# A 7-stage transformer block pair on one core: one phase order for all Winograd quads, a raised estimate of accumulating DMAs, splits three units ahead, squares summed on VectorE, gate tiles in the other row

## The chip, the core and the metric

The kernel runs on one core of a Trainium2 chip. Its engines each work through a queue of their own in order: TensorE (PE; PEld is its weight load), VectorE (DVE), ScalarE (ACT), GpSimd (POOL) and SyncE (SP), which only issues transfers. They are coupled by semaphores. The metric is the device time of one execution in microseconds; lower is better. All weights stay in HBM and are streamed through on-chip memory once.

## The reference

All arithmetic is fp32, for a sequence of 512 tokens with 1024 channels. Two blocks run one after the other. Cut to its main lines:

```python
h = x + concat(gla(n), mla(n)) @ w_out             # n = rms_norm(x); stage mix
h = h + square(relu(rms_norm(h) @ w_mlp_up)) @ w_mlp_down      # mlp: 1024 -> 4096 -> 1024
h = h + (p @ w_ple_proj) * sigmoid(rms_norm(h) @ w_ple_gate + b)   # ple
x = h
x = x + pool_mixer(rmsnorm(x))                     # pool: trailing means
x = x + conv_ffn(rmsnorm(x), ...[0])               # ffn0: 1024 -> 2816 -> 1024
x = x + chunk_attention(rmsnorm(x))                # att
x = x + conv_ffn(rmsnorm(x), ...[1])               # ffn1

def conv_ffn(h):
    a = h @ w_gate
    a = causal_depthwise_conv3(a) + conv_b
    return (silu(a) * (h @ w_val)) @ w_out
```

The change is in the three stages mlp, ffn0 and ffn1.

## The kernel before

`x` is kept transposed as 8 tiles of 128 channels by 512 tokens. A stage's norm doesn't scale its input: the products run on `x` times the gain, and each product is multiplied by the row `R` (one over the root mean square of each token) when it leaves PSUM. `square` sums the squares of the 8 tiles (`sq`), `stats` turns the sum into `ms` (a matmul `pst`, then VectorE), `r` (POOL's power), `dg` (ACT), `psr` (a matmul) and `R` (ACT).

**Weights.** They come in units of 128x1024 fp32 (512 KB). SP loads a unit into one of 7 slots `ws`. `split_unit` makes two float32r tiles of it: ACT copies two halves of 128x512 to `wh`, VectorE takes `wl` = `ws` - `wh`. There are 4 such pairs, so the split of unit n needs the pair of unit n-4, which TensorE must have finished. Each product is three matmuls (`mm3`): high by high, low by high, high by low. `splitter` runs at most `lazy` units ahead of TensorE's current one.

**Quads.** The up products of mlp, ffn0 and ffn1 take four feature tiles at a time (a Quad) by a Winograd scheme with seven products instead of eight. They are named in PHASES by position: 0 b11, 1 b21, 2 n3, 3 n2, 4 n1, 5 b22, 6 t4. Each is one unit and 24 matmuls of 128x256 into a PSUM tile `pq0` to `pq4`. n3, n2 and b22 share one `ws` tile ("sum"): SP loads source block 0, a DMA on POOL's queue adds block 2 for n3, and after n3's split another adds block 3 for n2, and after n2's split a third adds block 1 for b22. n1's tile ("low") is a load and one accumulating DMA. On the input side b11 and b22 use the tile's halves `xs`, n3 and n2 use `xc`, t4 uses `xt`. Copies `c1`, `u2`, `u4` by ACT take partial results out of `pq0`, so the next phase that needs `pq0` waits for them.

The order of the phases in a quad was one of three tuples at line 55: FIRST for a stage's first quad, LAST for the last quad of each ffn, MOST for all others (`quads[q].order`, line 1264). The first four feature tiles of a stage are done plainly (`first_tiles`, PSUM tiles `pf`, four units of 24 matmuls 128x512). After each group of quads come its downs: `pdn`, units of 24 matmuls that take the activations `y` (as `yh`, `yl`); `units_quads` places them between phases of the next group's quads, after the positions in the tuple at line 1267.

**ffn rows.** A quad's results make two rows of two tiles: row 0 is complete at the last position, row 1 one position earlier. In `finish` (line 1614) row 0 is the gate (convolution in `fb`, then Silu) and row 1 the value, which is multiplied with it to `y`.

**What sets the order.** The program is written by tasks with priorities (`spawn`, `drive`). `Pace` estimates when each engine and tile is free, `drive` takes the best task that could start by then, and the order so found is fixed in each engine's queue. An instruction that waits holds everything behind it on its engine. `Pace.note` (line 95) has an accumulating DMA's tile ready 4.8 us after its issue. All instructions are recorded through one helper and carry its line, L148, so they are told apart by their tiles.

Of the kernel before, what the change touches and what calls it, by code (L numbers as in the profile page):

```python
# [53 lines left out]

FIRST, MOST, LAST = (0, 1, 2, 3, 6, 4, 5), (2, 0, 1, 3, 6, 4, 5), (2, 0, 1, 3, 5, 4, 6)
# [17 lines left out]
class Pace:  # L73
# [21 lines left out]
    def note(self, engine, op, args, kw):  # L95
# [39 lines left out]
        for x in outs:  # L135
            self.ready[x.tensor.name] = start + cost + (2.0 if engine == "sync" else 4.8 if op == "dma_start" else 0.08)
# [22 lines left out]
class Norm:  # L159


    def __init__(self, gain):
        self.gain, self.xs, self.acc, self.count = gain, [None] * KD, None, 0
        self.ms = self.r = self.R = None
        self.low, self.blocks = [None] * 4, {p[0]: [None] * 4 for p in PHASES}
        self.plain = False
# [11 lines left out]
class Quad:  # L178


    def __init__(self, src):
        self.src, self.tile, self.order = src, {}, MOST


class Block:
# [86 lines left out]
    def plan_loads(self):  # L272

        self.loads, known = [], set()
        for n, u in enumerate(self.units):
            if not isinstance(u[0], str):
                self.loads.append((n, n, u[0], u[1], None, ()))
            elif u[1] not in known:
                known.add(u[1])
                for name, block, at, more in LOADS:  # L280
                    at = -5 if u[1].order == FIRST and name == "sum" else at
                    self.loads.append((n + at, u[1], u[1].src[block], 1024, name, more))
        self.loads.sort(key=lambda e: e[0])
# [203 lines left out]
    def square(self, norm, x, row=True, late=True):  # L487
        nc = self.nc
        sq = self.slot("sq")
        nc.scalar.activation(sq, x, AF.Square)  # L490
        if norm.acc is None:
            norm.acc = sq
        else:
            (nc.vector if late and norm.count > 5 else nc.gpsimd).tensor_add(norm.acc, norm.acc, sq)
        norm.count += 1
        if norm.count == KD:
            self.spawn(self.stats(norm, row), -4)
# [754 lines left out]
    def units_quads(plain, src, downs, sizes):  # L1252
# [3 lines left out]
        for g, n in enumerate(sizes):  # L1256
            for i in range(n):
                left -= 1
                if q < 0:
                    order.append((q, 0))  # L1260
                    units += plain
                else:
                    most = 0 if q == 0 else -(-len(wait) // (n - i)) if left else len(wait) - 2
                    quads[q].order = FIRST if q == 0 else MOST if left or most > 0 else LAST
                    for at, ph in enumerate(quads[q].order):
                        order.append((q, ph))
                        units.append(("quad", quads[q], ph))
                        for _ in range(((5, 2, 6, 3) if i else (5, 6, 4, 3))[:min(most, len(wait))].count(at)):
                            order.append(wait[0][:2])
                            units.append(wait.pop(0)[2])  # L1270
                q += 1
# [36 lines left out]
    def quads(self, norm, order, quads, sizes, last, after, take, finish, late=None):  # L1308
# [8 lines left out]
        for what, i in order:  # L1317
# [8 lines left out]
            own = quads[what].order != MOST  # L1326
# [26 lines left out]
            if i == quads[what].order[-1]:  # L1353
# [255 lines left out]
    def ffn(self, L, norm, after):  # L1609
# [4 lines left out]
        def finish(acts, rows, r, i):  # L1614
            f = 2 * count[r]
            count[r] += 1
            if r == 0:
                yield rows[0]
                made = []
                for w in range(2):  # L1620
                    a, b = rows[0][w], self.slot("fb")
# [10 lines left out]
            for w, b in enumerate(gates.pop((i, id(acts)))):  # L1632
                y = rows[1][w]
# [159 lines left out]
    def main(self, stages):  # L1793
# [13 lines left out]
        for i, st in enumerate(stages):  # L1807
# [11 lines left out]
            self.help = self.HELP[st in self.QUADS]  # L1819
            yield from run[st](norm, after)  # L1820
            self.lazy, self.most = self.LAZY[1], self.NL
# [88 lines left out]
def lay_out(x, p, positions, attn_norm, w_in, gla_gate_w2, gla_gate_b, gla_out_norm, mla_q_norm, mla_w_uq, mla_kv_norm,  # L1910
# [30 lines left out]
    for L in range(2):  # L1941
        both = np.stack([w.reshape(DM, -1, 2, P) for w in (ffn_w_gate_2[L], ffn_w_val_2[L])], 2)
# [45 lines left out]
```

## Time and profile before

| | us |
|---|---|
| median of 3 runs (lowest, highest) | 1703.4 (1700.95, 1705.31) |
| the profiled execution | 1700.45 |
| its span | 1698.7 |
| PE busy | 1638.1 (96%) |
| VectorE busy | 1260.0 (74%) |
| ACT busy | 887.4 (52%) |
| POOL busy | 280.1 (16%) |
| mean granted clock of TensorE | 0.983 of full speed |

In the timeline each row is: start in us, length in us, engine, line, operation, output <- input with size, count, and in brackets the idle time ahead of it and whose result ended it. A row with xN stands for N instructions, its length is from the first to the last.

### The profile page before, as it was taken

Reading aid. Unit: us, or ns where it says so; the run is one execution under the profiler, and the core shown is the slowest. Engines: PE = TensorE matmul, PEld = TensorE weight load, DVE = VectorE, ACT = ScalarE, POOL = GpSimd, SP = SyncE. Lnnn points to the kernel's source line nnn. Section 1 sums busy time; section 2 is a strip of 40 time slices with the busy share of each in tenths; the row PEclk is TensorE's granted clock in tenths of the full one; section 3 lists DMA queues with packets and bytes.
Section 4 is the critical chain, followed back from the end, with each engine's and each line's share of the span. In section 5 each row is a group of like instructions: output and inputs, shape, how many; then the busy total and the mean of one; then the engine's idle time right before and its main releaser. Section 6 shows DMA issues by size and latency. Waiting matters only on the chain. (4 is left out here: it accounts for less than half of the span.)

```text
span 1698.7 us, 27854 instructions
## 1 busy us (share of the span) xinstructions
PE 1638.1 (96%) x10676; PEld 1467.1 (86%) x10676; DVE 1260.0 (74%) x2435; ACT 887.4 (52%) x1730; POOL 280.1 (16%) x310
## 2 busy tenths in 40 slices
PE   9999999999999999979999998999999989999998
PEld 7878778899999888869999997998988779999987
DVE  7976868766666667878787767576668788787766
ACT  6745456544444465654454534476666554455532
POOL 3432302100000022211011100321322211111100
PEclk9999999999999999979999998999999989999999
DMA  7101223556666333366777753322231467777741
GB/s 275 50 26 38 98 77 100 158 160 164 165 164 174 134 99 116 82 155 174 186 187 183 180 156 107 120 83 68 76 100 63 112 164 184 176 201 180 184 128 50
DMA packets 66391, 224.87 MB, mean 132 GB/s; under 512 B 7617, under 2 KB 9554, under 8 KB 66258
## 3 DMA queue, kind: packets, MB, share of 16 engines
q1 hardware_dynamic: 50706, 166.46, 28.0%
q0 software_dynamic: 15552, 56.63, 19.3%
q8 instruction: 84, 1.38, 0.3%
q14 instruction: 49, 0.40, 0.1%
HBM read 220.96 MB, written 2.10 MB: 131 GB/s over the span
## 5 line engine op out<-in xcount | busy, mean ns | idle before, releaser
L148 ACT ACTIVATE wh<-ws 128x512 fp32r<-128x512 f32 x690 | 392.1, 621 | 258.2 <-PE pdn L148 125.7
L148 DVE TENSOR_TENSOR wl<-ws,wh 128x512 fp32r<-128x512 f32 x667 | 437.4, 698 | 110.9 <-ACT wh L148 110.8
L148 PE MATMUL pq<-xsl,wh 128*128 128x256 f32 x864 | 244.5, 283 | 0.0
L148 PE MATMUL pq<-xsh,wl 128*128 128x256 f32 x864 | 244.5, 283 | 0.0
L148 PE MATMUL pq<-xsh,wh 128*128 128x256 f32 x864 | 244.4, 283 | 0.0
L148 DVE TENSOR_TENSOR x<-x,pdn 128x512 f32<-128x512 f32 x177 | 119.8, 680 | 78.3 <-PE pdn L148 77.9
L148 POOL DMA_DIRECT2D ws<-in_w_f x80 | 70.6, 937 | 611.7 <-DVE wl L148 279.2
L148 PEld LDWEIGHTS pq<-xsh,wh 128*128 128x128 f32 x864 | 165.7, 192 | 1.3
L148 PEld LDWEIGHTS pq<-xsl,wh 128*128 128x128 f32 x864 | 165.6, 192 | 1.2
L148 PEld LDWEIGHTS pq<-xsh,wl 128*128 128x128 f32 x864 | 165.6, 192 | 0.0
L148 PE MATMUL pdn<-yh,wh 128*128 128x512 f32 x352 | 142.9, 406 | 14.8 <-ACT yh L148 14.7
L148 PE MATMUL pdn<-yl,wh 128*128 128x512 f32 x352 | 142.8, 406 | 5.7 <-DVE yl L148 5.6
L148 PE MATMUL pq<-xch,wh 128*128 128x256 f32 x432 | 126.5, 293 | 15.2 <-ACT wh L148 9.6
L148 PE MATMUL pdn<-yh,wl 128*128 128x512 f32 x352 | 140.8, 400 | 0.0
L148 PE MATMUL pq<-xch,wl 128*128 128x256 f32 x432 | 125.4, 290 | 0.4 <-DVE wl L148 0.4
L148 PE MATMUL pq<-xcl,wh 128*128 128x256 f32 x432 | 125.0, 289 | 0.0
L148 PE MATMUL paq<-wh,xsh 128*128 128x256 f32 x384 | 111.3, 290 | 1.9 <-DVE akk L148 1.2
L148 PE MATMUL paq<-wl,xsh 128*128 128x256 f32 x384 | 108.6, 283 | 0.0
L148 PE MATMUL paq<-wh,xsl 128*128 128x256 f32 x384 | 108.5, 283 | 0.0
L148 PEld LDWEIGHTS pq<-xch,wh 128*128 128x128 f32 x432 | 85.8, 199 | 18.1 <-ACT wh L148 10.8
L148 PE MATMUL pdn<-hh,wh 128*128 128x512 f32 x256 | 99.9, 390 | 0.0
L148 PE MATMUL pdn<-hl,wh 128*128 128x512 f32 x256 | 99.9, 390 | 0.0
(332 smaller groups left out, 3941.3 us busy)
## 6 DMA issues: line engine op xcount, KB each, us to landing
ws<-in_w_f SPq DMA_DIRECT2D x108, 512.0 KB, 3.8
ws<-in_w_f POOLq DMA_DIRECT2D x80, 512.0 KB, 5.5
ws<-in_w_fo SPq DMA_DIRECT2D x44, 512.0 KB, 4.8
ws<-in_w_up SPq DMA_DIRECT2D x39, 512.0 KB, 3.8
ws<-in_w_down SPq DMA_DIRECT2D x32, 512.0 KB, 4.1
ws<-in_w_up POOLq DMA_DIRECT2D x28, 512.0 KB, 5.8
ws<-in_w_out SPq DMA_DIRECT2D x8, 512.0 KB, 3.2
ws<-in_w_gate SPq DMA_DIRECT2D x8, 512.0 KB, 3.2
```

The costliest lines, as they stand in the source:

```text
L148: return call(*args, **kw)
```

## The change

Six edits. One tuple ORDER = (2, 0, 1, 3, 6, 4, 5) takes the place of FIRST, MOST and LAST; what hung on the order (an own PSUM tile for b22 in the first and the last quad, the early load in the first) hangs on two flags. The planner takes 7.0 us instead of 4.8 for an accumulating DMA. In mlp, ffn0 and ffn1 `lazy` is 3 instead of 2. In the norms of these stages VectorE adds all squares; POOL had added the first ones. In the ffns gate and value are packed the other way round, so the gate is row 1. In quad 1 of the ffns (the first quad with downs of the plain tiles) the downs stand after positions 5 and 6 rather than 2 and 5.

```diff
@@ -51,8 +51,7 @@
 PHASES = (("b11", 0, True, "a11"), ("b21", 1, True, "a12"), ("n3", 2, True, "sum"), ("n2", 0, False, "sum"),
           ("n1", 0, False, "low"), ("b22", 0, False, "sum"), ("t4", 3, True, "a22"))
 
-
-FIRST, MOST, LAST = (0, 1, 2, 3, 6, 4, 5), (2, 0, 1, 3, 6, 4, 5), (2, 0, 1, 3, 5, 4, 6)
+ORDER = (2, 0, 1, 3, 6, 4, 5)
 
 LOADS = (("sum", 0, -3, (2,)), ("a11", 0, 1, ()), ("a12", 1, 2, ()), ("low", 2, 2.5, (3,)), ("a22", 3, 4, ()))
 
@@ -133,7 +132,7 @@
                 if x.tensor.name in self.open:
                     self.open[x.tensor.name] = (self.step, start + cost + 0.08)
         for x in outs:
-            self.ready[x.tensor.name] = start + cost + (2.0 if engine == "sync" else 4.8 if op == "dma_start" else 0.08)
+            self.ready[x.tensor.name] = start + cost + (2.0 if engine == "sync" else 7.0 if op == "dma_start" else 0.08)
 
 
 class Engine:
@@ -161,6 +160,7 @@
 
     def __init__(self, gain):
         self.gain, self.xs, self.acc, self.count = gain, [None] * KD, None, 0
+        self.only = gain in ("mlp_norm", "ffn0", "ffn1")
         self.ms = self.r = self.R = None
         self.low, self.blocks = [None] * 4, {p[0]: [None] * 4 for p in PHASES}
         self.plain = False
@@ -179,7 +179,7 @@
 
 
     def __init__(self, src):
-        self.src, self.tile, self.order = src, {}, MOST
+        self.src, self.tile, self.first, self.own = src, {}, False, False
 
 
 class Block:
@@ -278,7 +278,7 @@
             elif u[1] not in known:
                 known.add(u[1])
                 for name, block, at, more in LOADS:
-                    at = -5 if u[1].order == FIRST and name == "sum" else at
+                    at = -5 if u[1].first and name == "sum" else at
                     self.loads.append((n + at, u[1], u[1].src[block], 1024, name, more))
         self.loads.sort(key=lambda e: e[0])
 
@@ -491,7 +491,7 @@
         if norm.acc is None:
             norm.acc = sq
         else:
-            (nc.vector if late and norm.count > 5 else nc.gpsimd).tensor_add(norm.acc, norm.acc, sq)
+            (nc.vector if late and (norm.count > 5 or norm.only) else nc.gpsimd).tensor_add(norm.acc, norm.acc, sq)
         norm.count += 1
         if norm.count == KD:
             self.spawn(self.stats(norm, row), -4)
@@ -1261,11 +1261,12 @@
                     units += plain
                 else:
                     most = 0 if q == 0 else -(-len(wait) // (n - i)) if left else len(wait) - 2
-                    quads[q].order = FIRST if q == 0 else MOST if left or most > 0 else LAST
-                    for at, ph in enumerate(quads[q].order):
+
+                    quads[q].first, quads[q].own = q == 0, q == 0 or left + most == 0
+                    for at, ph in enumerate(ORDER):
                         order.append((q, ph))
                         units.append(("quad", quads[q], ph))
-                        for _ in range(((5, 2, 6, 3) if i else (5, 6, 4, 3))[:min(most, len(wait))].count(at)):
+                        for _ in range(((5, 2, 6, 3) if i and q > 1 else (5, 6, 4, 3))[:min(most, len(wait))].count(at)):
                             order.append(wait[0][:2])
                             units.append(wait.pop(0)[2])
                 q += 1
@@ -1323,7 +1324,7 @@
                 yield from self.first_tiles(norm, take, acts[0])
                 continue
             block, acc, first, _ = PHASES[i]
-            own = quads[what].order != MOST
+            own = quads[what].own
             if i == 5 and own:
                 acc, first = 4, True
             if quad is None:
@@ -1350,7 +1351,7 @@
             self.used(ps[acc])
             if i != 2:
                 self.spawn(self.quad_step(i, ps, quad, own), -3)
-            if i == quads[what].order[-1]:
+            if i == ORDER[-1]:
                 ps = quad = None
 
     def quad_step(self, i, ps, quad, own):
@@ -1614,11 +1615,11 @@
         def finish(acts, rows, r, i):
             f = 2 * count[r]
             count[r] += 1
-            if r == 0:
-                yield rows[0]
+            if r == 1:
+                yield rows[1]
                 made = []
                 for w in range(2):
-                    a, b = rows[0][w], self.slot("fb")
+                    a, b = rows[1][w], self.slot("fb")
                     s.activation(b, a, AF.Identity, scale=cw[2](f + w), bias=self.col(f"cb{L}", f + w))
                     yield [b]
                     v.scalar_tensor_tensor(b[:, 1:], a[:, :T - 1], cw[1](f + w), b[:, 1:], op0=OP.mult, op1=OP.add)
@@ -1630,7 +1631,7 @@
                 return
             yield lambda: (i, id(acts)) in gates
             for w, b in enumerate(gates.pop((i, id(acts)))):
-                y = rows[1][w]
+                y = rows[0][w]
                 yield [b, y]
                 self.mul(y, y, b)
                 yield [y]
@@ -1817,8 +1818,9 @@
                 nxt = None
                 after = self.store
             self.help = self.HELP[st in self.QUADS]
+            self.lazy = self.LAZY[st not in ("mix", *self.QUADS)]
             yield from run[st](norm, after)
-            self.lazy, self.most = self.LAZY[1], self.NL
+            self.most = self.NL
             norm = nxt
 
 
@@ -1939,7 +1941,7 @@
     o["w_proj"] = np.ascontiguousarray(proj.reshape(2, 4, P, 256).transpose(0, 2, 1, 3)).reshape(2, P, 1024)
     o["w_pool"] = np.ascontiguousarray(pool_w_2[0].reshape(2, 2, 2, P, 256).transpose(0, 3, 1, 2, 4)).reshape(2, P, 1024)
     for L in range(2):
-        both = np.stack([w.reshape(DM, -1, 2, P) for w in (ffn_w_gate_2[L], ffn_w_val_2[L])], 2)
+        both = np.stack([w.reshape(DM, -1, 2, P) for w in (ffn_w_val_2[L], ffn_w_gate_2[L])], 2)
         o[f"w_f{L}_0"], o[f"w_f{L}"] = pack_first(both[:, 0]), pack_quads(both[:, 1:])
         o[f"w_fo{L}"] = pack_downs(ffn_w_out_2[L], 2, QG2)
     q, k, v = np.split(attn_wqkv_2[0], 3, axis=1)
```

POOL's queue around the start of ffn0, before: `sq` are sums of squares, `ws_6653` is the "sum" tile of quad 0 (second and third accumulate), `ws_7237` that of quad 1, `ws_7411` its "low", `ws_7644` the "sum" of quad 2.

```order
L148 TENSOR_TENSOR sq_7168<-sq_7168,sq_7207 128x512
L148 DMA ws_7237<-in_w_f0 128x1024
L148 TENSOR_TENSOR sq_7168<-sq_7168,sq_7247 128x512
L148 TENSOR_TENSOR sq_7168<-sq_7168,sq_7264 128x512
L148 TENSOR_TENSOR sq_7168<-sq_7168,sq_7280 128x512
L148 DMA ws_7411<-in_w_f0 128x1024
L148 TENSOR_TENSOR r_7453<-ms_7451,mhalf_72 128x4
L148 DMA ws_6653<-in_w_f0 128x1024 x2
L148 DMA ws_7644<-in_w_f0 128x1024
L148 DMA ws_7237<-in_w_f0 128x1024 x2
```

The same place of POOL's queue after: `ws_6653` is again quad 0's "sum", `ws_7236` quad 1's, `ws_7421` its "low", `ws_7647` quad 2's "sum".

```order
L147 TENSOR_TENSOR xn_7187<-xn_7187 128x256
L147 TENSOR_TENSOR xn_7211<-xn_7211 128x256
L147 DMA ws_7236<-in_w_f0 128x1024
L147 DMA ws_6653<-in_w_f0 128x1024
L147 DMA ws_7421<-in_w_f0 128x1024
L147 TENSOR_TENSOR r_7471<-ms_7469,mhalf_72 128x4
L147 DMA ws_6653<-in_w_f0 128x1024
L147 DMA ws_7647<-in_w_f0 128x1024
L147 DMA ws_7236<-in_w_f0 128x1024 x2
```

The second accumulate of quad 0's "sum" (for n2) moved ahead of `r`; the second of quad 1's still stands behind the first of quad 2's.

ACT's queue at the same place, before: `wh_7469` is the split of n3, `wh_7567` of n2, `wh_7638` of b22; `R` is the norm's row.

```order
L148 ACTIVATE wh_7469<-ws_6653 128x512 x2
L148 ACTIVATE xsh_7164<-xn_7170 128x256
L148 ACTIVATE xsh_7180<-xn_7187 128x256
L148 ACTIVATE xsh_7203<-xn_7211 128x256
L148 ACTIVATE xsh_7243<-xn_7251 128x256
L148 ACTIVATE dg_7506<-ident_65,r_7453 128x128 x4
L148 ACTIVATE c1_7514<-pq0_7465 128x512
L148 ACTIVATE R_7559<-psr_7557 128x512
L148 ACTIVATE wh_7567<-ws_6653 128x512 x2
L148 ACTIVATE wh_7574<-ws_7053 128x512 x2
L148 ACTIVATE wh_7582<-ws_6976 128x512 x2
L148 ACTIVATE u2_7626<-pq0_7465 128x512
```

And after: `wh_7473` is the split of n2 (n3's, `wh_7312`, stands further ahead), `wh_7513` of t4, `wh_7556` of n1, `wh_7641` of b22, `wh_7650` of the next quad's n3.

```order
L147 ACTIVATE wh_7473<-ws_6653 128x512 x2
L147 ACTIVATE xsh_7164<-xn_7170 128x256
L147 ACTIVATE xsh_7180<-xn_7187 128x256
L147 ACTIVATE xsh_7203<-xn_7211 128x256
L147 ACTIVATE xsh_7247<-xn_7255 128x256
L147 ACTIVATE wh_7513<-ws_7053 128x512 x2
L147 ACTIVATE dg_7542<-ident_65,r_7471 128x128 x4
L147 ACTIVATE c1_7554<-pq0_7512 128x512
L147 ACTIVATE wh_7556<-ws_6976 128x512 x2
L147 ACTIVATE R_7603<-psr_7601 128x512
L147 ACTIVATE u2_7626<-pq0_7512 128x512
L147 ACTIVATE wh_7641<-ws_6653 128x512 x2
```

The splits of n2, t4 and n1 moved ahead of `R`.

PE's queue in quad 1 of ffn0, before, at the end of b21 (`pq1`):

```order
L148 MATMUL pq1_7812<-xsl_7326,wh_7733 128x256
L148 MATMUL pq1_7812<-xsh_7325,wl_7734 128x256
L148 MATMUL pdn_7839<-yh_7867,wh_7774 128x512
L148 MATMUL pdn_7839<-yl_7868,wh_7774 128x512
L148 MATMUL pdn_7839<-yh_7867,wl_7775 128x512
```

The same place after; `wh_7841` is n2's.

```order
L147 MATMUL pq1_7804<-xsl_7345,wh_7709 128x256
L147 MATMUL pq1_7804<-xsh_7344,wl_7710 128x256
L147 MATMUL pq0_7773<-xch_7377,wh_7841 128x256
L147 MATMUL pq0_7773<-xcl_7378,wh_7841 128x256
L147 MATMUL pq0_7773<-xch_7377,wl_7842 128x256
```

The first down moved from ahead of n2 to behind n1. Around ffn0's first quad PE's order by units was `pf`, `pst`, `pf`, b11, b21, n3 (18 matmuls), `psr`, n3, n2, t4, n1, b22 and is `pf`, `pst`, n3, b11, b21, n2 (15), `psr`, n2, t4, n1, b22; in ffn1 `psr` now stands in t4, after 12.

ACT's queue in the last quad of ffn1, before: `wh_17880` is the split of n2, `wh_17917` of b22.

```order
L148 ACTIVATE wh_17880<-ws_17426 128x512 x2
L148 ACTIVATE yh_17890<-qr_17668 128x512
L148 ACTIVATE wh_17917<-ws_17426 128x512 x2
L148 ACTIVATE c1_17926<-pq0_17879 128x512
L148 ACTIVATE yh_17928<-qr_17669 128x512
```

And after: `wh_17862` is n2's, `wh_17899` t4's, `wh_17932` n1's, `wh_17963` b22's.

```order
L147 ACTIVATE wh_17862<-ws_17407 128x512 x2
L147 ACTIVATE yh_17882<-qr_17578 128x512
L147 ACTIVATE wh_17899<-ws_17636 128x512 x2
L147 ACTIVATE c1_17930<-pq0_17895 128x512
L147 ACTIVATE wh_17932<-ws_17599 128x512 x2
L147 ACTIVATE wh_17963<-ws_17407 128x512 x2
```

The copy `c1` moved ahead of b22's split.

## Rows read from the trace of the kernel before

**Rows 1.** The page: busy time by engine, and the granted clock in 40 slices.

```profile
PE 1638.1 (96%) x10676; PEld 1467.1 (86%) x10676; DVE 1260.0 (74%) x2435; ACT 887.4 (52%) x1730; POOL 280.1 (16%) x310
...
PEclk9999999999999999979999998999999989999999
```

**Rows 2.** Waits of PE: us in total, times, longest.

```profile
PE pdn L148 <- ACT yh L148: 14.7, 5, 7.2
```

**Rows 3.** Timeline of PE, the matmuls that end its idle stretches.

```profile
298.59 0.39 PE L148 MATMUL pq<-xch,wh 128*128 128x256 f32 x1 [1.82 <-ACT wh L148]
...
719.08 1.12 PE L148 MATMUL psr<-dg,ones 128*128 128x512 f32 x2 [1.46 <-ACT dg L148]
...
724.50 0.39 PE L148 MATMUL pq<-xch,wh 128*128 128x256 f32 x1 [3.58 <-ACT wh L148]
...
753.98 0.79 PE L148 MATMUL pdn<-yh,wh 128*128 128x512 f32 x1 [7.25 <-ACT yh L148]
...
1022.08 0.58 PE L148 MATMUL pq<-xch,wh 128*128 128x256 f32 x1 [2.74 <-ACT c L148]
...
1358.26 0.58 PE L148 MATMUL pq<-xch,wh 128*128 128x256 f32 x1 [4.18 <-ACT wh L148]
...
1385.67 0.80 PE L148 MATMUL pdn<-yh,wh 128*128 128x512 f32 x1 [4.71 <-ACT yh L148]
```

**Rows 4.** Windows of PE alone: length, busy (matmuls), granted clock, DMA share, GB/s.

```profile
724.45:728.60 4.15, 3.89 (x19) 0.59 0.21 25
1022.00:1026.50 4.50, 4.42 (x25) 0.64 0.57 179
1358.20:1363.60 5.40, 5.34 (x25) 0.54 0.39 61
...
753.90:765.20 11.30, 9.32 (x24) 0.62 0.58 128
...
1385.60:1396.55 10.95, 9.42 (x24) 0.62 0.69 145
```

**Rows 5.** The chain that ended last, in ffn1: start, us, what.

```profile
1351.15 6.40 DMA ws<-in_w_f
1359.83 5.71 DMA ws<-in_w_f
...
1367.60 3.24 DMA ws<-in_w_f
1371.94 10.25 DMA ws<-in_w_f
...
1396.60 8.63 PE pq L148 x72
1405.23 5.47 PE pdn L148 x24
```

**Rows 6.** Timeline of ACT in ffn0's quad 1 and ffn1's last quad.

```profile
748.91 2.19 ACT L148 ACTIVATE wh<-ws 128x512 fp32r<-128x512 f32 x4 [4.42 <-DMA ws<-in_w_f]
...
1651.84 1.15 ACT L148 ACTIVATE wh<-ws 128x512 fp32r<-128x512 f32 x2 [6.29 <-DMA ws<-in_w_f]
1652.89 0.58 ACT L148 ACTIVATE c<-pq 128x512 f32<-128x512 f32 x1
```

**Rows 7.** POOL's issues of accumulating DMAs: timelines, and the page's landing times.

```profile
737.97 1.75 POOL L148 DMA_DIRECT2D ws<-in_w_f  x2 [11.03 <-DVE u L148]
...
ws<-in_w_f POOLq DMA_DIRECT2D x80, 512.0 KB, 5.5
```

**Rows 8.** Timelines of VectorE and POOL ahead of ffn0, where squares are added.

```profile
695.27 2.29 DVE L148 SCALAR_TENSOR_TENSOR xc<-xn 128x256 f32<-128x256 f32 x1
...
701.02 0.68 DVE L148 TENSOR_TENSOR sq<-sq 128x512 f32<-128x512 f32 x1
701.63 0.41 DVE L148 SCALAR_TENSOR_TENSOR xc<-xn 128x256 f32<-128x256 f32 x1
...
695.67 4.48 POOL L148 TENSOR_TENSOR sq<-sq 128x512 f32<-128x512 f32 x3
```

## The prediction

> **What bounds the kernel now.** I read the page's busy shares and slices first: TensorE is busy for 96% of the span, and its granted clock dips in only a few slices [rows 1]. So there are two ways to gain: stop an idle stretch of TensorE, or stop the half-speed stretch that follows one. The profiled execution took 1700.45 us (span 1698.7), the median of the three runs is 1703.4; the sum below stands against 1700.45, and since the median is 2.95 above it, I treat a shift of 3 us as uncertain either way. About 0.3%, 5 us, is what a measurement can tell from no change.
>
> The list of TensorE's waits has the downs that wait for ACT's `yh` at its head, 14.7 us in five places [rows 2]. The timeline of TensorE shows where [rows 3]: not in the steady quads, but at the edges of the three quad stages. At 298.59 (mlp's first quad), 724.50 (ffn0's) and 1358.26 (ffn1's) phase n2 starts 1.82, 3.58 and 4.18 us late for its split. At 719.08 `psr` waits 1.46. At 753.98 and 1385.67 the first down of the ffns waits 7.25 and 4.71. At 1022.08 the last quad's n2 waits 2.74 for the copy `c1`, and the last quad of ffn1 does the same.
>
> After each wait the clock falls. The windows over the units behind the waits have a granted clock of 0.54 to 0.64 [rows 4], where the long steady stretches of the chain have 72 matmuls 128x256 in 8.63 us, 0.12 each, and a down's 24 in 5.47 [rows 5]; the level in the slow part is 1.2 GHz instead of 2.4. So ffn0's n2 took 3.89 for 19 matmuls instead of 2.28 (+1.6), ffn1's 5.34 for 25 instead of 3.0 (+2.3), the last quad's 4.42 for 25 (+1.4). The two downs' windows are 11.30 and 10.95 long instead of 5.47: 5.8 and 5.5 more, clock and small gaps inside together.
>
> **The change part by part: what it removes.**
> (a) One order for all quads. n2 needs the tile of n3 after a further accumulating DMA, and that starts only when n3 has been split. With n3 directly ahead of n2 there is no room for it: ffn1's chain shows that DMA from 1351.15 for 6.40 us, n2 right behind it [rows 5]. n3 now stands two phases earlier, and its split three units ahead, so POOL issues n2's DMA ahead of `r` (the order shows it). Two more phases, 5.8 us, plus the issue ahead of `r` exceed every one of the three waits. Gone: 1.8 (mlp), 3.6+1.6 (ffn0), 4.2+2.3 (ffn1).
> (b) `psr` moves from 18 matmuls into the third quad unit to 15 into the fourth; `pf`'s last six matmuls move ahead of it. Net distance behind `pst`: 72+15 against 6 wide ones and 66, so 10.4 us instead of about 9.3; its wait of 1.46 goes for the most part: 1.5. In ffn1 it moves on into t4, where nothing waited before.
> (c) First down of the ffns. ACT sat for 4.42 us in front of a split that waited for an accumulating DMA, at 748.91 [rows 6], and the `yh` that the down needs stood behind it. Now the down comes after n1' instead of ahead of n2', three phases (8.6 us) later; the gate's rows are complete one phase earlier, so its chain over ACT and VectorE runs earlier too. 7.25+5.8 and 4.71+5.5 go: 13.1+10.2 = 23.3.
> (d) Last quads of the ffns: ACT's `c1` copy stood behind a split that had waited 6.29 for its third accumulate, at 1651.84, and was issued at 1652.89 [rows 6]; in the new order the copy is ahead of it and t4 and n1 lie between n2 and b22. 2.74+1.4, twice: 8.2.
> Sum removed: 1.8+5.2+6.5+1.5+23.3+8.2 = 46.5.
>
> **What it adds.**
> (e) A new wait in quad 1 of each ffn. With the down gone from between b21' and n2', TensorE arrives at n2' at once. The order shows n2's second DMA behind the sum DMA of quad 2 in POOL's queue, as before, and that one needs a slot which b22's split of quad 0 frees, then a load (3.24 us at 1367.60), then POOL [rows 5]. Behind the waiting split on ACT are the splits of t4', n1' and the first down, then `yh`; behind POOL's waiting issue stands n2's. In before the pair was issued at 737.97 in ffn0 and n2's part had landed when the split at 748.91 began, 10.9 us on; in ffn1 it took 10.25 [rows 5 to 7].
> Price for ffn1: TensorE stood free at 1385.67−4.71 = 1380.96; with 6.5 taken out above it arrives at 1374.4. The DMA landed at 1371.94+10.25 = 1382.2, with 1.3 for the split 1383.5. If nothing in that chain moved, the gap is 9.1. If it moved by the whole link that n2's DMA was in (1359.83−1351.15 = 8.7), the gap is 0.4. The order puts b22's split behind `R`, six scalings and one subtraction on VectorE, and `R` comes later than before, so half of the link: about 5. For ffn0 the same chain gains the larger wait and I take 4. Then the clock: as behind 1358.26, 2.3 each. Added: 4+5+4.6 = 13.6; bounds 1 to 23.
> (f) Fifteen adds of squares move from POOL to VectorE, five per stage: 5 x 0.68 = 3.4 us more per stage, if nothing else changes [rows 8]. Against it: while POOL had its three adds of 4.48 us, an `xc` step of VectorE took 2.29 instead of 0.41, 1.9 more beside three adds [rows 8]. For five adds that is 3.1 back if all do so: bounds 0.3 to 3.4 lost per stage on VectorE. TensorE sees it only through `xc` for n3 (now the first phase) and through `ms`, where (b) leaves about 1 us of margin. I take 0 and keep +10 in all three stages for the range.
> The Trainium skill ("SBUF — State Buffer", Who interferes with whom) says that a VectorE instruction with two SBUF inputs and a GpSimd one that reads SBUF exclude each other; the stretched `xc` row agrees with it; by it (f) would come out even, while the 7 `xn` subtractions that move to POOL would each hold VectorE up once.
> (g) Estimate 7.0 instead of 4.8, and two scalings on ACT instead of VectorE: no instruction is added; they only set the order, which is what (c) and (d) rest on. The accumulating DMAs' median is 5.5 [rows 7], so the planner now puts splits a little late rather than early: cost 0, at most the 1 us that a late split could add in a place where slack is thin. Splits three ahead need a `wh`/`wl` pair that TensorE frees one unit earlier, so ACT waits at most for the unit before: nothing, unless it blocks copies (third rival).
>
> Net: −46.5+13.6 = −32.9; 1700.45−32.9 = 1667.5, so 1667.
>
> **The rivals.**
> First, n2' is hidden: the pair lands 5 us sooner because fewer loads run beside it (a single one takes 5.5 [rows 7], not 10.3). Then nothing is added: 1700.45−46.5 = 1654. For: single landings of 5.5. Against: the two pairs above took twice that.
> The Trainium skill ("DMA: Bandwidth & Descriptors", Anatomy of one DMA — SWDGE (gpsimd) path) gives 2.0 us plus bytes/436e3, an estimate of 3.2 for 512 KB; by that the pair would be in time and this rival would hold. The trace's 5.5 and 10.3 speak against it.
> Second, the first down still waits. Its four `y` come one after another from a chain ACT-VectorE-ACT, and the new wait at n2' also holds the splits ahead of `yh`. If the windows' excess of 5.8 and 5.5 stays although the first wait goes, 11.3 comes back: 1679; with (e) at its upper bounds 1688.
> Third, slower: splits three ahead put ACT, in the 20-odd middle quads too, in front of a split whose DMA hasn't landed, with `c1` or `u2` behind it, as at 1651.84. Each costs 2.74+1.4 = 4.1. Eight such quads eat the gain, ten make it slower by over 5; all 20 give 1667+82 = 1749. Against: the steady quads show no wait now, `c1` moves ahead of those splits where I see it, and the raised estimate makes the planner more careful.
> Fourth, the change doesn't do what it says: the planner's order and the real times differ, the n2 waits only move on to `psr` and t4. Half of 46.5 gone with (e) in full leaves −10: 1690.
>
> **How the numbers follow.** Forecast (1659 to 1675) 0.62; first rival (1650 to 1659) 0.15; second (1675 to 1688) 0.13; fourth (1688 to 1698) 0.05; third 0.05, of which 0.04 is slower by over 5. The range 1652 to 1688 takes the forecast, most of the first and the second, and the bounds of (e) and half of (f). Faster by over 0.3%: 0.94; within: 0.02; slower: 0.04.
>
> **What would show it.** In the changed trace: no wait of n2 in the first quads and no wait of the last quads' n2; the first down starting within 2 us of n1'; a wait of 3 to 6 us at n2' of quad 1 in both ffns with a dip of the clock behind it; VectorE busy by some 5 to 10 us more, POOL by less. The prediction is wrong if middle quads show waits, if `psr` or n3 wait in the ffns for more than 2 us, or if n2' doesn't wait.

## The result, and the profile after

The changed kernel takes 1676.9 us (median of four runs, 1676.23 to 1677.87) against 1702.89 before: a ratio of 0.9847 with a 95% interval of 0.983 to 0.9864, 26 us less. The profiled execution's span is 1675.1 instead of 1698.7. The forecast was 1667.

The page of the changed kernel, first TensorE's and the other engines' busy time, then the granted clock in 40 slices (both answer [rows 1]):

```profile
PE 1633.1 (97%) x10676; PEld 1463.3 (87%) x10676; DVE 1249.1 (75%) x2441; ACT 890.3 (53%) x1732; POOL 265.5 (16%) x302
...
PEclk9999999999999999999999999999999999999999
```

TensorE is busy for 5.0 us less with the same 10676 matmuls, at a mean granted clock of 0.988 instead of 0.983, so this is half-speed time that is gone; the other 18.6 us of the span is idle time that is gone. VectorE, which took over 15 adds, is busy for 10.9 us less; the prediction had expected 5 to 10 more.

TensorE's waits after (us in total, times, longest), for [rows 2]:

```profile
PE pdn L147 <- ACT yh L147: 8.2, 7, 4.0
PE pq L147 <- ACT wh L147: 6.3, 2, 4.2
PE pdn L147 <- DVE yl L147: 4.0, 7, 1.2
...
PE pq L147 <- ACT c L147: 1.0, 2, 0.6
```

Where they are, in the timeline of TensorE (start, length, what, and in brackets the idle time and its releaser), for [rows 3]:

```profile
714.81 0.39 PE L147 MATMUL pq<-xch,wh 128*128 128x256 f32 x1 [0.35 <-ACT c L147]
...
738.11 0.48 PE L147 MATMUL pq<-xch,wh 128*128 128x256 f32 x1 [2.03 <-ACT wh L147]
...
782.94 0.50 PE L147 MATMUL pdn<-yh,wh 128*128 128x512 f32 x1 [0.86 <-ACT yh L147]
784.64 0.50 PE L147 MATMUL pdn<-yl,wh 128*128 128x512 f32 x1 [1.20 <-DVE yl L147]
...
1034.11 0.49 PE L147 MATMUL pdn<-yh,wh 128*128 128x512 f32 x1 [4.03 <-ACT yh L147]
...
1364.58 0.58 PE L147 MATMUL pq<-xch,wh 128*128 128x256 f32 x1 [4.25 <-ACT wh L147]
...
1409.21 0.50 PE L147 MATMUL pdn<-yh,wh 128*128 128x512 f32 x1 [0.86 <-ACT yh L147]
```

All the rows of [rows 3] are gone (a prime, as in n2', marks a phase of quad 1): of the first quads' n2 waits 0.35 is left, in ffn0, `psr` doesn't wait, the first down of quad 1 doesn't wait, nor do the last quads' n2. What is there instead: n2 of quad 1 (738.11 and 1364.58), which was forecast, and something that was not: the first down of quad 2 (782.94 and 1409.21). Each has a stretch of the lower clock behind it. The windows over these units (length, busy with count, granted clock, DMA share, GB/s), first the quad products, then the downs, for [rows 4]:

```profile
738.10:743.00 4.90, 4.86 (x26) 0.65 0.38 52
1364.50:1370.10 5.60, 5.53 (x26) 0.53 0.47 77
```

```profile
780.50:793.30 12.80, 9.57 (x24) 0.73 0.73 164
...
1406.80:1418.70 11.90, 9.51 (x24) 0.71 0.78 173
```

A down of 24 matmuls takes 5.47 undisturbed [rows 5]; here 12.8 and 11.9. So quad 2's first downs cost 7.3 and 6.4 us, together more than the difference between the forecast and the time (9.9).

**Where the down of quad 2 loses it.** ACT's queue in ffn0 (timeline), for [rows 6]:

```profile
760.05 0.82 ACT L147 ACTIVATE fb<-qr,cols 128x512 f32<-128x512 f32 x1 [1.87 <-DVE qr L147]
769.07 1.15 ACT L147 ACTIVATE wh<-ws 128x512 fp32r<-128x512 f32 x2 [8.21 <-DMA ws<-in_w_f]
...
771.17 0.57 ACT L147 ACTIVATE c<-pq 128x512 f32<-128x512 f32 x1
...
772.69 0.62 ACT L147 ACTIVATE fb<-fb 128x512 f32<-128x512 f32 x1
773.21 0.80 ACT L147 ACTIVATE fb<-qr,cols 128x512 f32<-128x512 f32 x1
```

At 760.05 ACT starts quad 1's gate. Its Silu (`fb<-fb`) could follow when VectorE's convolution is done, 766.66 in VectorE's timeline; it runs at 772.69, because ACT stood for 8.21 us in front of quad 2's n2 split. Why that split waits, the chain of the same stretch shows (start, us, what):

```profile
750.51 1.02 DVE wl L147 x2
...
752.43 4.98 DMA ws<-in_w_f
...
757.97 0.54 POOL ws L147
758.51 10.46 DMA ws<-in_w_f
...
769.07 0.09 ACT wh L147
```

POOL's timeline at the same place:

```profile
757.97 1.77 POOL L147 DMA_DIRECT2D ws<-in_w_f  x2 [7.92 <-DVE x L147]
```

VectorE's `wl` frees a slot, SP loads quad 3's "sum" into it (4.98), POOL issues that tile's first accumulate and behind it, in the same moment, n2's for quad 2 (POOL's row has both). The second of the pair has landed 10.46 us later, where the median of all 80 in the ffns is 5.4. POOL's DMA queue (q0) moved 144 packets between 757 and 763.3, none until 764.4 and 144 after that, so the second's transfer began only when the first's was done. So n2's DMA was held twice, by a load that it doesn't need and by a transfer that it doesn't need.

### The profile page after: what moved, and what is told of

Read it like the earlier page. It is cut to its first block, busy times and chain, and to the rows that moved or that the text cites. A ratio compares the mean times of both kernels' runs of the same rounds, so it can differ in the third digit from the quotient of the medians.

```text
span 1675.1 us, 27870 instructions
## 1 busy us (share of the span) xinstructions
PE 1633.1 (97%) x10676; PEld 1463.3 (87%) x10676; DVE 1249.1 (75%) x2441; ACT 890.3 (53%) x1732; POOL 265.5 (16%) x302
## 4 chain that ended last, share of the span: by engine, by line
PE 82%; DVE 9%; DMA 3%; ACT 3%; issue 2%; POOL 0%; SPq 0%; DVEq 0%; ACTq 0%; POOLq 0%
PE pq L147 31%; PE pdn L147 24%; PE paq L147 7%; PE pw L147 5%; PE pf L147 4%; DMA ws<-in_w_f 2%; PE pgv L147 2%; DVE wl L147 2%; PE ao L147 1%; PE at L147 1%; DVE gqt L147 1%; PE pg L147 1%; ACT aqh L147 1%; PE msc L147 1%; PE asc L147 1%
## 5 line engine op out<-in xcount | busy, mean ns | idle before, releaser
L147 PE MATMUL pdn<-hh,wl 128*128 128x512 f32 x256 | 99.6, 389 | 0.0
```

The source lines that it names most:

```text
L147: return call(*args, **kw)
```

## The experiments

All kernels start from the changed one ("after") unless the text says otherwise. The table has the medians, the ratio to before with its interval, and what TensorE took in each stage of the profiled execution, from the first matmul of a stage's plain tiles (`pf`) to the next stage's first one (in ffn1 to TensorE's last). The stretches between are left out: the one from mlp to ffn0 takes 80.0 before, 78.8 in after, e3_lazy2 and e7_late_lazy2, and 79.9 to 80.5 in the others; the one from ffn0 to ffn1 takes 257.9 or 258.0 in all. The mix column (from the start to mlp's first `pf`) varies by 3.6 us between kernels in which nothing of it is edited, so a difference of medians of up to 3 us is not told apart unless the stages show it. The profiled execution is one of the four, and in e2_est48, e5_order1 and e6_gate0 the longest of them, 3.8, 2.7 and 3.4 us above the median.

| kernel | us | ratio (interval) | mix | mlp | ffn0 | ffn1 |
|---|---|---|---|---|---|---|
| before | 1703 | 1 | 264.4 | 342.0 | 377.3 | 373.0 |
| after | 1676.9 | 0.9847 (0.983, 0.9864) | 264.6 | 339.2 | 366.6 | 363.7 |
| e1_lateadd | 1655.55 | 0.9718 (0.9701, 0.9735) | 264.6 | 339.2 | 355.2 | 350.7 |
| e2_est48 | 1680.19 | 0.9862 (0.9841, 0.9883) | 264.5 | 339.2 | 369.1 | 366.9 |
| e3_lazy2 | 1667.41 | 0.9787 (0.977, 0.9804) | 265.0 | 339.2 | 363.0 | 360.0 |
| e4_down2 | 1675.62 | 0.9835 (0.982, 0.9849) | 264.2 | 339.2 | 364.7 | 364.3 |
| e5_order1 | 1675.57 | 0.9832 (0.9815, 0.9848) | 266.8 | 340.3 | 365.1 | 362.2 |
| e6_gate0 | 1680.03 | 0.9861 (0.9841, 0.988) | 267.5 | 339.2 | 365.5 | 366.9 |
| e7_late_lazy2 | 1651.8 | 0.9698 (0.9683, 0.9712) | 264.8 | 339.2 | 353.1 | 350.7 |
| e8_before_late | 1689.29 | 0.9914 (0.9899, 0.9929) | 265.9 | 344.8 | 370.1 | 366.4 |
| e9_order1_late | 1665.05 | 0.977 (0.9753, 0.9788) | 264.6 | 340.2 | 358.8 | 357.0 |
| e10_sqpool | 1680.18 | 0.9858 (0.9839, 0.9877) | 263.9 | 339.2 | 367.7 | 363.9 |
| e11_ll_sqpool | 1654.63 | 0.9707 (0.9689, 0.9724) | 264.6 | 340.2 | 353.8 | 353.1 |
| e12_ll_est48 | 1651.14 | 0.9687 (0.9672, 0.9703) | 263.9 | 339.2 | 353.0 | 350.8 |

### The queue of accumulating DMAs

Theory A: POOL's in-order queue, and ACT's behind it. Theory B: long transfers under load, and a y chain that is too long. e1_lateadd queues an accumulate only when its load is due by the planner:

```diff
+    def added(self, quad, name, more, t):
+        if more:
+            yield [t]
+        for block in more:
+            self.nc.gpsimd.dma_start(t, quad.src[block], accum_op=OP.add)
+        quad.tile[name] = t
...
-                n.tile[name] = t
-                for block in more:
-                    self.nc.gpsimd.dma_start(t, n.src[block], accum_op=OP.add)
+                self.spawn(self.added(n, name, more, t), -9)
```

> Changed kernel, with one thing more: the accumulating DMA of a sum or low tile is put into POOL's queue only when its load is due by the planner's estimate, not right behind the load's issue; so n2's accumulate of quad 1 stands ahead of quad 2's sum accumulate instead of behind it. Theory A (POOL's queue holds n2's accumulate behind one that waits for a load, and ACT's queue holds the y chain behind the split that waits for it): the waits of n2 in quad 1 (2.0 and 4.3 us) and of quad 2's first down in both ffns go with their half-speed stretches, 3.8+6.8+7.1+6.3 = 24 us at most, 1653 to 1660. Theory B (the tile lands 11 us late because loads run beside it, and the y chain is simply too long for quad 2's first down): the waits stay, 1670 to 1680.

Measured: 1655.55, 21.4 less than after. In POOL's queue of e1_lateadd (timeline) n2's accumulate for quad 2 goes out first, released by that tile's own split, and quad 3's "sum" 2.4 us later, released by its load; in after the two went out as one pair. On ACT the split of quad 2's n2 waits for TensorE alone, and the Silu comes right behind it:

```profile
749.55 0.87 POOL L147 DMA_DIRECT2D ws<-in_w_f  x1 [5.72 <-DVE wl L147]
751.97 0.88 POOL L147 DMA_DIRECT2D ws<-in_w_f  x1 [1.54 <-DMA ws<-in_w_f]
...
759.65 1.15 ACT L147 ACTIVATE wh<-ws 128x512 fp32r<-128x512 f32 x2 [1.79 <-PE pdn L147]
761.20 0.64 ACT L147 ACTIVATE fb<-fb 128x512 f32<-128x512 f32 x1 [0.40 <-DVE fb L147]
```

No n2 waits any more in its trace, and of the first downs of quad 2 only 0.99 us each is left. Theory A holds, B falls: the transfers themselves have the same median (5.5 against 5.4 in after), and the two ffns take 11.4 and 13.0 us less, which is what the four waits with their dips cost.

e8_before_late puts the same edit into the kernel before.

> Kernel before with the late queueing of accumulating DMAs alone. Theory: POOL's queue is behind the first down's wait in the kernel before too (ACT's 4.42 us in front of a split), so most of step (c), 23 us, goes, and the waits of n2 in first quads with n3 directly ahead of it and of the last quads stay: 1703.8-20 = 1684 (1678 to 1690). Rival: the late queueing acts only together with the new order: 1697 to 1706.

Measured: 1689.29, some 14 less than before, at the edge of the theory's band. In ffn0 and ffn1 it brings 7.2 and 6.6, in mlp it loses 2.8. So POOL's queue had a part in the waits of the kernel before too; the last quads' n2 waits stay (2.98 and 2.87), as the theory has it. Its other half fails: the n2 waits of the first quads, 1.82, 3.58 and 4.18 in [rows 3], mostly go too, although n3 stands directly ahead of n2 as before. What is left of them is 0.56 in mlp, 0.23 in ffn0 (for `wl`) and 1.24 in ffn1 (for `c1`):

```profile
299.20 0.39 PE L148 MATMUL pq<-xch,wh 128*128 128x256 f32 x1 [0.56 <-ACT wh L148]
...
1353.84 0.39 PE L148 MATMUL pq<-xch,wh 128*128 128x256 f32 x1 [1.24 <-ACT c L148]
```

Other waits stand beside them (`psr` 1.71 and 1.16, further phases of the first quads 1.96 and 1.68), so the 14 us aren't step (c) alone.

### The order alone, and the order with the queue

e5_order1 is the kernel before with the one ORDER and nothing else of the change.

> Kernel before with the one phase order alone (and the flags that replace the tuples); estimate 4.8, splits two ahead, squares, gate rows and downs as before. Theory A: the order alone removes the waits of n2 in the first quads and of the last quads, steps (a), (b) and (d) of the prediction, 1.8+5.2+6.5+1.5+8.2 = 23, and the first down still waits for yh behind the split that waits for quad 1's n2 accumulate: 1703.8-23 = 1681 (1676 to 1688). Rival: without the estimate and the third unit the planner puts n2's split behind R as before and little of it goes: 1690 to 1700.

Measured: 1675.57, just under theory A's band, which can't be told from the whole change (1676.9). The other five edits, taken together, bring nothing here. It isn't that they do nothing: the waits are other ones. In e5_order1 b22 of quad 0 waits for its split, and matmuls of quad 1's first down for their y (TensorE's timeline):

```profile
732.76 0.41 PE L147 MATMUL pq<-xsh,wh 128*128 128x256 f32 x1 [3.78 <-ACT wh L147]
...
747.29 0.50 PE L147 MATMUL pdn<-yl,wh 128*128 128x512 f32 x1 [0.77 <-DVE yl L147]
...
751.60 0.80 PE L147 MATMUL pdn<-yh,wh 128*128 128x512 f32 x1 [3.58 <-ACT yh L147]
```

Against after: 1.5 less in each ffn, 1.1 more in mlp, 2.2 more in the mix and 1.5 more between mlp and ffn0. The last quads' n2 doesn't wait; of the other waits that the order was to remove, 0.78 is left at mlp's first n2 (for `c1`) and 0.75 at ffn1's `psr`.

e9_order1_late adds the late queueing to that.

> Kernel before with the one phase order and the late queueing of accumulating DMAs, none of the other five edits. Theory: the order and POOL's queue are the two causes, and the other edits only treat what POOL's queue does; then 1651 to 1657, as with them (1651.8 with splits two ahead). Rival: without the downs of quad 1 moved and the gate completed first, the first down waits for y in both ffns (it stands right behind b21'), 4 to 8 us each with a dip of 2 to 4: 1664 to 1675.

Measured: 1665.05, in the rival's band, though not with the rival's waits: the longest at quad 1's first down is 2.69, in ffn0, and in ffn1 it is quad 2's first down that waits (1.27). With the queue mended, the four other edits (estimate, squares, downs, gate) are worth 13.3 us together, since e7_late_lazy2 below has them beside the same order, queue and splits two ahead, and takes 1651.8. In e9_order1_late TensorE's downs wait for y in many small pieces (us, times, longest):

```profile
PE pdn L147 <- DVE yl L147: 6.3, 6, 2.7
PE pdn L147 <- ACT yh L147: 5.2, 7, 1.3
```

In e7_late_lazy2 these are 5.8 instead of 11.5. Of the four, undone alone there, the squares are 2.8 (e11_ll_sqpool, intervals overlapping) and the estimate nothing (e12_ll_est48), so by difference some 10 would be the downs' and the gate's, which no run undoes there. In after that gain doesn't show (e4_down2, e6_gate0), as the wait for the accumulate is there with either.

### Splits three units ahead

```diff
-            self.lazy = self.LAZY[st not in ("mix", *self.QUADS)]
+            self.lazy = self.LAZY[st != "mix"]
```

> Changed kernel with splits two units ahead again in the quad stages. If the third unit is what gives n2's accumulate its head start over r at the start of the ffns, n2 of quad 0 waits again by 2 to 4 us with its dip: 1681 to 1692. If n3 standing two phases ahead is enough, within 3 us of 1676.9.

Measured: 1667.41, 9.5 us less than after by the medians and 7.2 by the profiled spans (3.6 and 3.7 in the two ffns), and on neither expectation: the third unit costs. e3_lazy2's ACT queue at the same place as above:

```profile
767.02 0.63 ACT L147 ACTIVATE fb<-fb 128x512 f32<-128x512 f32 x1 [3.10 <-DVE fb L147]
767.56 0.80 ACT L147 ACTIVATE fb<-qr,cols 128x512 f32<-128x512 f32 x1
774.13 2.19 ACT L147 ACTIVATE wh<-ws 128x512 fp32r<-128x512 f32 x4 [5.77 <-DMA ws<-in_w_f]
```

The split still waits 5.77 us for its accumulate, but the Silu and the next gate stand ahead of it now, and quad 2's first down doesn't wait at all. n2 of quad 1 still waits (3.05 and 3.44), as POOL's queue is the same. The late tile was there all the time; splitting three ahead put the y chain behind it.

e7_late_lazy2 has both.

> Accumulating DMAs queued when their load is due (as in the run e1_lateadd, 1655.55), with splits two units ahead. Theory: the third unit hurt only by standing on ACT in front of the y chain while it waited for a late accumulate (1676.9 against 1667.4 without it); with the accumulates in time there is nothing to wait for and both are equal: 1652 to 1659. Rival: a third unit ahead costs by itself, through ACT's and VectorE's queues: 1646 to 1651.

Measured: 1651.8, 3.7 less than e1_lateadd (the intervals, 0.9683 to 0.9712 and 0.9701 to 0.9735, just overlap), at the theory's edge: with the accumulates in time the third unit costs at most a few us instead of 9.5. By the stages 2.1 of it is in ffn0, whose last downs wait 4.04 in e1_lateadd and 0.40 and 2.43 here, none in ffn1, and 1.7 is between mlp and ffn0. Its page and waits of downs:

```profile
PE 1620.5 (98%) x10676; PEld 1456.2 (88%) x10676; DVE 1251.1 (76%) x2441; ACT 887.6 (54%) x1732; POOL 271.6 (16%) x302
```

```profile
PE pdn L147 <- DVE yl L147: 3.9, 3, 2.4
...
PE pdn L147 <- ACT yh L147: 1.9, 4, 0.5
```

What is left in the quad stages is the last downs of the ffns.

### The other edits, undone one at a time

The downs of quad 1 back after positions 2 and 5:

```diff
-                        for _ in range(((5, 2, 6, 3) if i and q > 1 else (5, 6, 4, 3))[:min(most, len(wait))].count(at)):
+                        for _ in range(((5, 2, 6, 3) if i else (5, 6, 4, 3))[:min(most, len(wait))].count(at)):
```

> Changed kernel with the downs of quad 1 in the ffns back after positions 2 and 5. The prediction's step (c) says the first down then waits for yh: the trace of the changed kernel has the first yh at 741.6 in ffn0, while b21' ends at 736.1, so 5.5 us and more for the following y, with the dip 10 to 12 per ffn; n2' no longer waits (3.8 and 6.8 back). Sum 1676.9+21-10.6 = 1687 (1682 to 1692). Rival: the y chain was late only behind the split on ACT, and moves up with it: then the down covers n2' and the time is 1666 to 1672.

Measured: 1675.62, no difference, between the two. The first downs wait as step (c) has it:

```profile
742.50 0.79 PE L147 MATMUL pdn<-yh,wh 128*128 128x512 f32 x1 [5.88 <-ACT yh L147]
...
1369.21 0.79 PE L147 MATMUL pdn<-yh,wh 128*128 128x512 f32 x1 [9.73 <-ACT yh L147]
```

The expectation counted only n2' as what comes back; quad 2's first down doesn't wait either in e4_down2, so the one wait just takes the place of the two others. This confirms (c)'s reason for moving the downs, and that it gains nothing as long as the late accumulate only moves the wait on.

Gate and value in their old rows (the lines of `finish` and the packing as in before):

> Changed kernel with gate and value in their old rows (gate complete with the last phase). Theory A: the y chains are held by ACT's wait for quad 2's n2 split and not by the row's time, so within 4 us of 1676.9. Rival (the row order is what gets the y in time): the gate's convolution starts 2.9 us later in each quad, quad 1's and quad 2's first downs and the tails of both ffns wait that much more, with their dips: 1685 to 1695.

Measured: 1680.03, 3.1 more than after. The profiled span is 6.6 longer: 2.9 in the mix column and 1.7 between mlp and ffn0, both ahead of anything that the edit touches, 1.1 less in ffn0, 3.2 more in ffn1. Not told apart from no effect: the theory's side, if weakly.

The estimate back at 4.8:

```diff
-            ... 7.0 if op == "dma_start" else 0.08)
+            ... 4.8 if op == "dma_start" else 0.08)
```

> Changed kernel with the planner's estimate of accumulating DMAs back at 4.8 us. If the estimate is what keeps splits from standing ahead of copies on ACT (the prediction's view of the last quads), the last quads' n2 or the middle quads wait again and the time is 1681 to 1690. If the phase order alone does that, it is within 3 us of 1676.9. POOL's order at quad 1 is the same, so n2' waits as in the changed kernel by both.

Measured: 1680.19, on neither expectation. The medians' intervals overlap; by the stages of the profiled execution, the longest of its four, 2.5 and 3.2 us are lost in the ffns. The waits differ more than the time: quad 2's first down is free, but n2' waits behind the copy `c1`, and quad 1's first down in ffn1 waits:

```profile
742.79 0.58 PE L147 MATMUL pq<-xch,wh 128*128 128x256 f32 x1 [4.99 <-ACT c L147]
...
1380.53 0.80 PE L147 MATMUL pdn<-yh,wh 128*128 128x512 f32 x1 [6.08 <-ACT yh L147]
```

The last quads' n2 doesn't wait, so it was the order and not the estimate that freed them. Where the accumulates are in time the estimate is indifferent:

> Late queueing and splits two ahead (1651.8) with the estimate of accumulating DMAs at 4.8. If the estimate matters by itself, ACT again stands in front of splits whose tile isn't there, and copies or y wait: 1655 to 1665. If 7.0 only made room for what POOL's queue added to a DMA's time, within 3 us of 1651.8.

Measured: 1651.14 against 1651.8, the second case. This is the fastest kernel of the study, together with e7_late_lazy2; the two are equal.

The squares back on POOL:

```diff
-        self.only = gain in ("mlp_norm", "ffn0", "ffn1")
+        self.only = False
```

> Changed kernel with the sums of squares back on POOL (all but the last two adds). Step (f) of the prediction took their move at 0, bounds 0 to 10 lost by it; by that 1667 to 1677. Rival, the adds beside VectorE's work stretch it, as the xc row showed, and the accumulates behind them on POOL come later: 1680 to 1690.

> Late queueing and splits two ahead (e7_late_lazy2, 1651.8) with the sums of squares back on POOL: the same question where no accumulate waits. By step (f) within 2 us of 1651.8 (nothing waits for VectorE there); by the rival psr or n3 of the first quads waits for xc or r: 1655 to 1662.

Measured: 1680.18 and 1654.63, 3.3 and 2.8 more than with the squares on VectorE (the intervals overlap, both go the same way); the first in the rival's band, the second between the two. Of the profiled spans' 2.0 and 5.4, 1.6 and 1.7 lie between mlp and ffn0, where kernels without this edit differ as much, and 1.3 and 4.1 in the three stages. e10_sqpool's timelines ahead of ffn0: POOL's adds, VectorE beside them, and TensorE's first n3:

```profile
691.88 4.48 POOL L147 TENSOR_TENSOR sq<-sq 128x512 f32<-128x512 f32 x3
...
691.78 2.00 DVE L147 TENSOR_TENSOR xc<-xc,xn 128x256 f32<-128x256 f32 x1
693.70 1.51 DVE L147 TENSOR_TENSOR xn<-xn,xc 128x256 f32<-128x256 f32 x1
...
709.91 0.38 PE L147 MATMUL pq<-xcl,wh 128*128 128x256 f32 x1 [1.17 <-DVE xcl L147]
```

In after the same steps of VectorE, with its own adds between them:

```profile
692.81 0.42 DVE L147 TENSOR_TENSOR xc<-xc,xn 128x256 f32<-128x256 f32 x1
693.15 0.42 DVE L147 TENSOR_TENSOR xn<-xn,xc 128x256 f32<-128x256 f32 x1
694.15 0.69 DVE L147 TENSOR_TENSOR sq<-sq 128x512 f32<-128x512 f32 x1
```

Three adds on POOL took 4.48, and VectorE's steps beside them 2.00 and 1.51 instead of 0.42; VectorE does an add in 0.69. In all VectorE is busy for 1254.5 in e10_sqpool and 1249.1 in after, 5.4 less with 15 adds more (7 `xn` subtractions and two scalings of 0.4 to 0.5 leave it with them). No cost shows, and both runs point to a small gain.

## Why the prediction was right, and where it missed

By stage its own sum was −1.8 for mlp, −17.6 for ffn0 (5.2+1.5+13.1+4.1 removed, 6.3 added) and −13.5 for ffn1 (6.5+10.2+4.1 removed, 7.3 added). Measured between the two profiled executions: −2.8, −10.7 and −9.3, with 1.2 less ahead of ffn0. The time, 1676.9, is in the range 1652 to 1688 but above the forecast's own band (1659 to 1675); it fell into the second rival's, for a reason that this rival doesn't have, and that the range held is to that extent luck.

Of its own signs, those for the first quads, the last quads, the first down and POOL came true. VectorE's busy time went the other way, n2' of ffn0 waited less than 3 to 6 us, and "middle quads show waits" came true for quad 2.

- **(a), (b), (d)**, the phase order: right in mechanism and, as far as the rows tell, in size. All their waits are gone, and e5_order1 shows that the order alone does it but for 0.78 and 0.75. That there is no room for the DMA with n3 directly ahead of n2, the reason given in (a), doesn't hold in e8_before_late, where it stands so and ffn0's n2 hardly waits (0.23): late queueing, with the planner's order that comes of it, takes most of these waits away too.
- **(c)**, the first down: right for its place, 23.3 gone; e4_down2 puts the down back and finds the waits again (5.88 and 9.73). By the sum the move was worth 23.3−13.6 = 9.7 net of (e); e4_down2 does without it in the same time, since quad 2's first down then doesn't wait. That the gate's earlier row helps was argued there, and is not shown for after (e6_gate0); the downs' and the gate's edits may show their worth only with the queue mended (e9_order1_late against e7_late_lazy2, 13.3 us for these, the squares and the estimate).
- **(e)**, n2 of quad 1: right in place and mechanism, near in size: 2.03 and 4.25 instead of 4 and 5. The clock's part behind it, from the windows, is 1.7 (4.86 for 26 matmuls, 3.12 at 0.12 each) and 2.4 (5.53), against 2.3 each; in sum 10.4 for 13.6. e1_lateadd shows the cause, POOL's order, by removing it.
- **(f)**, taken at 0 with bounds on the side of a loss: the runs point to some 3 us of gain, twice the same way though each within the intervals. The loss of 0.3 to 3.4 us per stage on VectorE had the wrong sign: what VectorE lost beside POOL's adds was more than the one stretched `xc` row that was weighed against them, and the move takes 5.4 off its busy time (1254.5 in e10_sqpool, 1249.1 in after). The Trainium skill's rule ("SBUF — State Buffer", Who interferes with whom), that a VectorE instruction with two SBUF inputs and a GpSimd one that reads SBUF exclude each other, agrees with the rows of e10_sqpool: 2.00 and 1.51 beside POOL's adds, 0.42 without.
- **(g) is the step that failed.** "Splits three ahead ... nothing, unless it blocks copies": they cost 9.5 us (e3_lazy2; 7.2 in the profiled span). The prediction knew the mechanism, as its third rival, but looked for it in the 20 middle quads at 4.1 each, with copies behind the split, and gave it 0.05. It happened in quad 2 of the two ffns alone, with the y chain behind the split, at 7.3 and 6.4. That e3_lazy2's 1667.41 is the forecast's number is chance: its n2' and b22 wait (3.05, 3.44 and 1.67), and of its downs only the ffns' last ones do.
- **The second rival** has the right band (1675 to 1688) and the wrong down: quad 1's is free, quad 2's waits. The same late accumulate that (e) prices in quad 1 comes again one quad later, since the pair of quad 3's sum and quad 2's n2 stands in POOL's queue as well; the prediction followed POOL's order up to quad 1's pair and stopped there.
- **The first rival** rested on single transfers of 5.5; e1_lateadd makes n2's single (5.3 to 5.4 in ffn0's quads 1 and 2), and its 1655.55 is within 2 us of the rival's 1654. The Trainium skill's fit ("DMA: Bandwidth & Descriptors", Anatomy of one DMA — SWDGE (gpsimd) path), an estimate of 3.2 for 512 KB, is not borne out for these accumulating ones: 5.4 is the median in after.

Checked by sum: of −32.9, quad 2's first downs take back 13.7, and the end of ffn0 1.7 (the third of the last four downs starts 4.03 late, at 1034.11, and from the start of that wait to its end 14.0 us go by, where before it were 12.3); (e) was 3.2 smaller than priced. That gives −20.7; the profiled span shows −23.6. Of the 2.9 that stay, mlp has 1.0 and the stretch ahead of ffn0 1.2; they are not explained further.

## What to carry to other kernels

When a change moves an operation in one engine's queue, follow the waiting instruction's queue on for a whole further period of the loop, not only to the first place where it waits: here the same late tile stood in quad 1 and again in quad 2. An in-order queue that issues transfers should hold a transfer back until what it waits for is due; otherwise the next one, which could start, is held behind it, and then queues behind it in the transfer as well. And edits that treat the same wait can't be priced by undoing them one at a time: beside the order the five others together showed no gain, and four of them 13 us once the queue was mended.

## What the runs showed of the hardware that was not expected

When POOL issues two accumulating DMAs of 512 KB one right behind the other, the second has landed 10.46 us after its issue (758.51 in after's chain), and 10.25 in [rows 5], where the median of all 80 in the ffns is 5.4 to 5.5. In after there are 16 such pairs, and their second takes 7.27 to 10.46. It isn't always that one waits for the other: at 757.97 the first landed after 5.2 us and the second's packets followed behind it (144 up to 763.3, none until 764.4, 144 after), while at 1352.95 the first itself took 8.6 and packets of the second went before it had landed (199 of the 288 by 1361.6).

POOL's `r`, a power of 128x4, took 1.36 in after (711.60) and 4.56 in e1_lateadd (708.51), where VectorE was at work on `wl` and `xsl` from 708.34 on. No run separates the cause; spans on POOL are rough.
